# Transposes of a normalised token tile behind the next tile's matmuls, and the first products of the gated MLP interleaved over three units

## The chip, the core and the metric

One core of a Trainium2 chip runs the whole layer as one program. The metric is the device time of one execution in microseconds (us), of which the median of several runs counts. The engines each work through a queue of their own, in order: PE multiplies and transposes into banks of PSUM, ACT (ScalarE), DVE (VectorE) and POOL (GpSimd) do the elementwise work, and SP issues the DMA transfers. PE, ACT, DVE and POOL wait for each other only where one needs what another makes, or a buffer that another still uses.

## What is computed

The reference is one decoder layer on 1024 tokens of width 1024, in float32. The second half is the part that matters here:

```python
mix = jnp.concatenate([a_out, b_out], axis=-1)         # 1024 x 1024
x = x + rms_norm(mix @ w_out, norm_mix_post)
h = rms_norm(x, norm_ffn_pre)
g = jax.nn.gelu(causal_dwconv(h @ w_gate, conv_w, conv_b))   # width 2816
y = (g * (h @ w_up)) @ w_down
x = x + rms_norm(y, norm_ffn_post)
```

## The kernel before

The matrices are multiplied in parts: every operand is split into a high part (`fp32r`, written by ACT or DVE, L73 or L77) and a low part (the rest, L78, on DVE or POOL), and a product is three matmuls: high by high, high by low, low by high. One matmul is 128x128 by 128x512.

**The output projection.** The tokens are eight tiles of 128, taken in the order `TO` = 0, 1, 2, 3, 4, 6, 5, 7 (L682). For each tile, `wout_mm` issues 48 matmuls y (L622) into two banks. `wout_end` then normalises: ACT squares both halves (L698), POOL makes the statistics (L152, L157: n_7m and the first n_7r for tile 7), DVE scales (two L702) and adds x (L703), ACT squares the sum (L706), POOL makes the second statistics (L143, L145, again called n_7m and n_7r), and DVE scales the tile into xb (L708). `h2_trans` has PE transpose xb in eight 128x128 pieces (hT, L720), and ACT evacuates them with the gain (eight L725) into the tiles stg. `store_x1` stores the tile. In the loop the transposes of the previous tile stand before the last six of a tile's 48 matmuls (L1086).

**The gated MLP.** A unit is (gate or up, p): w_gate's or w_up's columns 256 p to 256 p + 255. Units come as g0, u0, g1, u1, ..., 22 in all; below, a, b and c are g0, u0 and g1, and 6a is product 6 of unit a. Each unit is one level of a fast matrix product with seven products, numbered 1 to 7; each is 12 matmuls (L845 to L847 in `prod`) with its own left side (hs, a split or a sum of stg, made by `hsplit` and `hs_sums`, L78 and L761 to L764) and its own weights (wtg or wtu, split by `wsplit`; the sums tg and tu of `tsums`, L795 to L798, two on POOL and two on DVE). Products 1 and 2 need only the even tiles (so tile 6 comes before tile 5), the others the odd ones too. The products go into banks A (1, then 2), B (6, then 7), C (5, then 3) and E (4), which the trace shows as Ag, Bg, Cg, Eg for gate units and Au, ... for up units. Between the two products of a bank `evac` reads the intermediate sum, and the second product has to wait for that. After product 3 of a gate unit `conv` does the convolution and GELU (L896 to L900), and `store_c` stores the result with four more sums for the down projection (sD, L911).

**What sets the order.** PE and SP run in the order of the code (`manual_schedule`); for ACT, DVE and POOL a scheduler chooses the order when the program is built, and from then on their queues are fixed. The order of the products is the list `SEQ`: of units a, b and c the products 1 and 2 of each, then 4a 4b, then the rest of a, the rest of b and the rest of c; from the fourth unit on `ORDER` = 1, 6, 2, 7, 5, 4, 3. Weights are split three products ahead (`LOOK`). Tile 7's transposes are called ahead of 1c, the fifth product. 32 buffers (mp, `mtile`) and 13 others (bg, `btile`) are handed around among all these tiles.

Of the kernel before, what the change touches and what calls it, by code (L numbers as in the profile page):

```python
# [34 lines left out]
NT = T // 128  # L35
# [27 lines left out]
def build(tc, x, g1, g2, g3, g4, w_in, ln_g, ln_b, sp_w, sp_b, rel, w_out, w_gate, w_up,  # L63
# [28 lines left out]
    with tc.manual_schedule(engines={ET.PE, ET.SP}), \  # L92
# [685 lines left out]
        def load_half(u):  # L778
            HALF[u] = btile("wh%s%d" % u).rearrange("p (k c) -> p k c", k=KT)
            sp.dma_start(HALF[u], (w_gate if u[0] == "g" else w_up)[:, u[1] * 256:u[1] * 256 + 128]  # L780
                         .rearrange("(k q) c -> q k c", q=128))

        def wblk(u, l, j):
            if u not in RW:
                return HALF[u][:, 4 * l:4 * l + 4, :]
# [74 lines left out]
        def evac(u, n):  # L860
# [197 lines left out]
        SEQ = [(u, n) for u in U[:3] for n in (1, 2)] + [(u, 4) for u in U[:2]]  # L1058
        SEQ += [(u, n) for u in U[:2] for n in (6, 7, 5, 3)] + [(U[2], n) for n in (6, 7, 5, 4, 3)]
# [12 lines left out]
        for c in range(1, NT):  # L1072
# [27 lines left out]
        hs_sums(2, 3)  # L1100
        for j in range(2, LOOK):
            wsplit(*SEQ[j])
        loaded = 2
        LS_ = len(SEQ)
        PRE = {LS_ - 5: lambda: [ahead_l(x, True) for x in range(2)], LS_ - 3: lambda: [ahead_l(x, True) for x in range(2, LL)],
               LS_ - 2: lambda: [ahead_s(x) for x in range(LS)]}
        for j, (u, n) in enumerate(SEQ):
            if j == 0:
                tsums(U[0])
            if j == 1:  # L1110
                tsums(U[1])
            if j == 4:
                h2_trans(NT - 1, bD)
                store_x1(NT - 1)
                for a in (4, 6, 7):
                    hsplit(a, 0, 3)
# [16 lines left out]
            if n == 7 and u[0] == "g" and u[1] > 0:  # L1133
# [93 lines left out]
```

## Time and profile before

| | us |
|---|---|
| median of 3 runs | 1215.32 (1213.35 to 1216.31) |
| profiled execution, its own time | 1219.78 |
| its span | 1218.1 |
| PE busy | 1163.5 (96%) |
| DVE busy | 840.5 (69%) |
| ACT busy | 581.8 (48%) |
| POOL busy | 368.1 (30%) |

PE's busy time counts matmuls as they overlap, so 96% is not 96% of its peak. The profile gives each engine's instructions with their start, what ended the idle time ahead of an instruction, and the TensorE clock granted in each stretch (1.00 is 2.4 GHz, 0.50 is 1.2 GHz). The output projection's tiles 1 to 7 lie between 470 and 562 us, the products of units a, b and c between 562 and 634 us, the remaining units up to about 1000 us, and the down projection behind them.

### The profile page before, as it was taken

To read this page: it belongs to the slowest core of one execution; us is meant where nothing else is said; L and a number is where in the kernel's file an instruction comes from. 1 tells how busy PE (TensorE), PEld (TensorE's weight loads), DVE (VectorE), ACT (ScalarE), POOL (GpSimd) and SP (SyncE) were. 2 spreads that over 40 slices of the span, in tenths; PEclk is the share of its full clock that TensorE was granted. 3 is DMA by queue.
4 is the path that set the end of the run, shared out by engine and by line. 5 is a ranking of instruction groups with operands and counts; after the bars stand their busy time and mean duration, and the time that the engine had idled before them with its cause. 6 is when DMAs were issued, how large, how long until landed. Compare 5 with 4: busy or idle time off the path is not lost.

```text
span 1218.1 us, 16548 instructions
## 1 busy us (share of the span) xinstructions
PE 1163.5 (96%) x5687; PEld 975.0 (80%) x5687; DVE 840.5 (69%) x1559; ACT 581.8 (48%) x1172; POOL 368.1 (30%) x401
## 2 busy tenths in 40 slices
PE   6899999999999999987899999999999999999996
PEld 4789978888887877875678888888888888888884
DVE  5752257777777785457777777677776779679665
ACT  4532156676765664445532434324343245445521
POOL 3850022333333473234023133221332220000342
PEclk9999999999998999999999999999999999999999
DMA  5314033433242232330223133231443279334336
GB/s 193 105 59 110 2 81 76 120 87 77 74 114 71 88 122 70 133 127 34 70 96 104 62 129 129 96 104 61 129 129 96 70 260 378 122 96 121 106 119 225
DMA packets 107562, 135.35 MB, mean 111 GB/s; under 512 B 30794, under 2 KB 74326, under 8 KB 107478
## 3 DMA queue, kind: packets, MB, share of 16 engines
q1 hardware_dynamic: 105318, 132.46, 34.9%
q10 hardware_dynamic: 2160, 1.84, 0.4%
q8 instruction: 45, 0.74, 0.3%
q14 instruction: 39, 0.32, 0.1%
HBM read 99.35 MB, written 35.71 MB: 111 GB/s over the span
## 4 chain that ended last, share of the span: by engine, by line
PE 77%; DVE 6%; issue 5%; POOL 5%; DMA 3%; ACT 2%; SPq 1%; POOLq 0%; DVEq 0%; ACTq 0%
PE d L986 15%; PE qk L471 10%; PE o L565 4%; PE pt L543 3%; PE s L511 2%; PE s L512 2%; PE v L240 2%; PE v L242 2%; PE v L241 2%; PE Bg L845 2%; PE Cu L845 2%; PE Bg L847 2%; PE Cu L846 2%; PE Cu L847 2%; PE Bg L846 2%
## 5 line engine op out<-in xcount | busy, mean ns | idle before, releaser
L986 PE MATMUL d<-t,s 128*128 128x512 f32 x924 | 210.3, 389 | 1.8 <-ACT t L73 1.5
L986 PEld LDWEIGHTS d<-t,s 128*128 128x128 f32 x924 | 173.3, 188 | 38.7 <-ACT t L73 1.9
L523 POOL TENSOR_SCALAR row<-row,rz 128x128 f32<-128x128 f32 (+3 forms) x96 | 72.8, 759 | 214.2 <-DVE rz L522 194.3
L520 ACT ACTIVATE row<-row,nm 128x128 f32<-128x128 f32 (+3 forms) x96 | 74.4, 775 | 48.9 <-DVE nm L515 48.6
L548 DVE TENSOR_TENSOR ptl<-pt,pth 128x512 fp32r<-128x512 f32 (+1 forms) x120 | 75.7, 634 | 20.1 <-ACT pth L547 18.5
L622 PE MATMUL y<-woh,ms 128*128 128x512 f32 x256 | 83.5, 398 | 1.5 <-POOL ms L78 1.1
L547 ACT ACTIVATE pth<-pt 128x512 fp32r<-128x512 f32 (+1 forms) x120 | 65.8, 550 | 34.0 <-PE pt L543 32.8
L471 PE MATMUL qk<-hTh,wqh 128*128 128x512 f32 x192 | 81.3, 423 | 0.0
L73 ACT ACTIVATE s<-sf 128x512 fp32r<-128x512 f32 x77 | 48.2, 627 | 66.4 <-PE d L986 26.1
L471 PE MATMUL qk<-hTl,wqh 128*128 128x512 f32 x192 | 78.9, 411 | 0.0
L471 PE MATMUL qk<-hTh,wql 128*128 128x512 f32 x192 | 76.9, 400 | 0.0
L78 DVE TENSOR_TENSOR s<-sf,s 128x512 fp32r<-128x512 f32 x77 | 56.5, 734 | 23.3 <-ACT s L73 23.1
L543 PE MATMUL pt<-ident,row 128*128 128x128 f32 x432 | 68.4, 275 | 1.8 <-POOL row L523 1.7
L1001 POOL TENSOR_TENSOR x<-x,g4t 128x512 f32<-128x512 f32 x12 | 18.8, 1577 | 162.1 <-DMA g4t<-in_norm_ffn_post 133.5
L73 ACT ACTIVATE wtg<-tg 128x512 fp32r<-128x512 f32 x44 | 27.5, 629 | 80.9 <-PE Cu L847 69.7
L898 DVE SCALAR_TENSOR_TENSOR c<-G,cols,c 128x1023 f32<-128x1023 f32 (+1 forms) x44 | 58.4, 1344 | 7.0 <-ACT c L896 7.0
L515 DVE CUSTOM_DVE_ANT_0 row<-s,bias 128x384 f32<-128x384 f32 (+2 forms) x96 | 49.8, 519 | 18.1 <-PE s L512 13.0
L543 PEld LDWEIGHTS pt<-ident,row 128*128 128x128 f32 x432 | 51.4, 140 | 10.7 <-POOL row L523 2.7
L73 ACT ACTIVATE wtu<-tu 128x512 fp32r<-128x512 f32 x44 | 27.6, 630 | 66.8 <-PE Cg L847 59.2
L795 POOL TENSOR_TENSOR tu<-wu 128x512 f32<-128x512 f32 x11 | 14.2, 1289 | 149.9 <-PE Ag L847 119.8
L622 PEld LDWEIGHTS y<-woh,ms 128*128 128x128 f32 x256 | 48.3, 189 | 12.2 <-POOL ms L78 1.6
L565 PE MATMUL o<-ptl,V 128*128 128x256 f32 x240 | 49.6, 288 | 4.8 <-DVE ptl L548 4.6
(334 smaller groups left out, 3224.4 us busy)
## 6 DMA issues: line engine op xcount, KB each, us to landing
sf<-sD SPq DMA_DIRECT2D x77, 256.0 KB, 2.8
wg<-in_w_gate SPq DMA_DIRECT2D x11, 1024.0 KB, 5.9
wu<-in_w_up SPq DMA_DIRECT2D x11, 1024.0 KB, 5.0
wd<-in_w_down SPq DMA_DIRECT2D x22, 512.0 KB, 7.1
sD<-c SPq DMA_DIRECT2D x30, 256.0 KB, 6.3
gcop<-gd SPq DMA_DIRECT2D x12, 576.0 KB, 4.6
wqk<-in_w_in SPq DMA_DIRECT2D x24, 256.0 KB, 5.5
bias<-gcop SPq DMA_DIRECT2D x12, 512.0 KB, 3.8
```

What stands on the lines that cost most here:

```text
L73: act.activation(hi, src, AF.Copy)
L78: lo_eng.tensor_sub(lo, src, hi.bitcast(F))
L471: pe.matmul(st[hf], w, m, start=k == 0 and j == 0, stop=k == KT - 1 and j == 2)
L520: act.activation(t[:, :w], t[:, :w], AF.Exp, bias=nm, scale=-1.0, accum_out=z)
L523: pool.tensor_scalar(t[:, :w], t[:, :w], rz, 1.0, op0=OP.mult, op1=OP.mult)
L543: pe.transpose(p[:, a * 128:(a + 1) * 128], r[:, jj * 128:(jj + 1) * 128], ident)
L547: act.activation(hi[:, :n], p[:, :n], AF.Copy)
L548: dve.tensor_sub(lo[:, :n], p[:, :n], hi.bitcast(F)[:, :n])
L565: pe.matmul(ov, v, t[:, s], start=j == 0 and x == 0, stop=x == 1 and j == 2 * g + 1, skip_group_check=True)
L622: pe.matmul(YP[i, hf], m, w, start=k == 0 and j == 0, stop=k == KT - 1 and j == 2)
L898: dve.scalar_tensor_tensor(c[:, d:T], g[:, 0:T - d], col(2 - d, f), c[:, d:T], op0=OP.mult, op1=OP.add)
L986: pe.matmul(b, l, r, start=first and n in FIRST and q == 0, stop=last and n in LAST and q == 2, skip_group_check=True)
```

## The change

1. In the loop over tiles the transposes (and the store, and the load of the next x) come after all 48 matmuls of the next tile, not before its last six. In the last pass they are left out: tile 5's now come ahead of the second product of the MLP. Tile 7's are called ahead of the fifth, as before.
2. The normalisation of tiles 5 and 7 and the transposes of both are put ahead in the scheduler's choice (`high_priority`).
3. The first 21 products alternate between units a, b and c (`HEAD`); the sums of stg, the splits and the sums of weights are called at other places in that list.
4. Unit c's weights come as two halves of 128 columns, and not as a half and then the whole. The sums tu of unit b take buffers of mp, not of bg.
5. `store_c` is called two products later; evacuations that waited for `conv` are done first in, first out, and may be of any product of an up unit.

```diff
-        def load_half(u):
+        def load_half(u, j):
-            HALF[u] = btile("wh%s%d" % u).rearrange("p (k c) -> p k c", k=KT)
+            HALF[u, j] = btile("wh%s%d_%d" % (u + (j,))).rearrange("p (k c) -> p k c", k=KT)
...
-                TW[key] = (btile if u in U[:2] else mtile)("t%s%d_%d" % (u + (a // 2,))).rearrange("p (a k c) -> p a k c", a=2, k=4)
+                TW[key] = (btile if u == U[0] else mtile)("t%s%d_%d" % (u + (a // 2,))).rearrange("p (a k c) -> p a k c", a=2, k=4)
...
-            if n == 2 and nm == "u" and p not in CONV:
+            if nm == "u" and p not in CONV:
                 LATE.append((u, n))
...
-        SEQ = [(u, n) for u in U[:3] for n in (1, 2)] + [(u, 4) for u in U[:2]]
-        SEQ += [(u, n) for u in U[:2] for n in (6, 7, 5, 3)] + [(U[2], n) for n in (6, 7, 5, 4, 3)]
+        HEAD = "1a 1b 2a 1c 2b 2c 4a 6a 6b 7a 5a 7b 3a 4b 6c 5b 7c 5c 3b 4c 3c".split()
+        SEQ = [(U["abc".index(x[1])], int(x[0])) for x in HEAD]
         SEQ += [(u, n) for u in U[3:] for n in ORDER]
...
-            for x_, f in enumerate(wout_mm(i, range(KT), bS if c % 2 else bD)):
-                if x_ == 42:
-                    h2_trans(TO[c - 1], bP)
-                    store_x1(TO[c - 1])
-                    if c + 1 < NT:
-                        load_xb(TO[c + 1])
-                    if c == 6:
-                        hsplit(1, 2, 4)
-                        hsplit(2, 2, 4)
+            for f in wout_mm(i, range(KT), bS if c % 2 else bD):
                 f()
-            wout_end(i)
+            if c < 6:
+                wout_end(i)
+            else:
+                with tc.high_priority(400):
+                    wout_end(i)
+            if c + 1 < NT:
+                h2_trans(TO[c - 1], bP)
+                store_x1(TO[c - 1])
+                load_xb(TO[c + 1])
+            if c == 6:
+                hsplit(1, 2, 4)
+                hsplit(2, 2, 4)
...
         for j, (u, n) in enumerate(SEQ):
-            if j == 0:
+            if j == 1:
+                with tc.high_priority(400):
+                    h2_trans(TO[NT - 2], bD)
+                store_x1(TO[NT - 2])
                 tsums(U[0])
-            if j == 1:
-                tsums(U[1])
+                hs_sums(2, 3)
+                hsplit(4, 0, 3)
+            if j == 2:
+                load_half(U[2], 1)
+                hsplit(6, 0, 3)
+                hsplit(7, 0, 3)
             if j == 4:
-                h2_trans(NT - 1, bD)
+                with tc.high_priority(400):
+                    h2_trans(NT - 1, bD)
                 store_x1(NT - 1)
-                for a in (4, 6, 7):
-                    hsplit(a, 0, 3)
                 hsplit(4, 3, 4)
                 hs_sums(3, 4)
                 hsplit(6, 3, 4)
                 hsplit(7, 3, 4)
+                tsums(U[1])
                 hsplit(5, 0, 4)
                 hsplit(3, 0, 4)
...
-            if n == 7 and u[0] == "g" and u[1] > 0:
+            if n == 4 and u[0] == "g" and u[1] > 0:
                 store_c(u[1] - 1)
```

Lines in the changed kernel move by one or two: L795 to L798 become L797 to L800, L845 becomes L847, L867 becomes L869, L896 to L900 become L898 to L902.

In the rows below, hT5 is the transposes of tile 5, hs4_1_0 the low part (1) of the first half (0) of the left side of product 4, wtg0_6 and wtu0_6 the weights of product 6 of units a and b (wtg1_6 of unit c), tg0 and tu0 the sums of a's and b's weights, yb7 and xb7 the tiles of token tile 7.

PE behind the last y of tile 7, before; the first matmul of each product is shown, eleven more follow it:

```order
L845 MATMUL Ag0_6364<-hs1_0_0_6124,wtg0_1_6338 128x512
...
L845 MATMUL Ag0_6364<-hs2_0_0_6132,wtg0_2_6341 128x512
...
L845 MATMUL Au0_6405<-hs1_0_0_6124,wtu0_1_6352 128x512
...
L845 MATMUL Au0_6405<-hs2_0_0_6132,wtu0_2_6361 128x512
...
L720 MATMUL hT7_0_6435<-ident_74,xb7_6213 128x128 x4
L720 MATMUL hT7_1_6444<-ident_74,xb7_6213 128x128 x4
L845 MATMUL Ag1_6517<-hs1_0_0_6124,wtg1_1_6385 128x512
...
L845 MATMUL Ag1_6517<-hs2_0_0_6132,wtg1_2_6402 128x512
...
L845 MATMUL Eg0_6552<-hs4_0_0_6454,wtg0_4_6420 128x512
...
L845 MATMUL Eu0_6568<-hs4_0_0_6454,wtu0_4_6514 128x512
...
L845 MATMUL Bg0_6586<-hs6_0_0_6462,wtg0_6_6532 128x512
```

The same place after the change:

```order
L847 MATMUL Ag0_6331<-hs1_0_0_6124,wtg0_1_6319 128x512
...
L720 MATMUL hT5_0_6346<-ident_74,xb5_6102 128x128 x4
L720 MATMUL hT5_1_6355<-ident_74,xb5_6102 128x128 x4
L847 MATMUL Au0_6390<-hs1_0_0_6124,wtu0_1_6322 128x512
...
L847 MATMUL Ag0_6331<-hs2_0_0_6132,wtg0_2_6325 128x512
...
L847 MATMUL Ag1_6443<-hs1_0_0_6124,wtg1_1_6328 128x512
...
L720 MATMUL hT7_0_6458<-ident_74,xb7_6239 128x128 x4
L720 MATMUL hT7_1_6467<-ident_74,xb7_6239 128x128 x4
L847 MATMUL Au0_6390<-hs2_0_0_6132,wtu0_2_6387 128x512
...
L847 MATMUL Ag1_6443<-hs2_0_0_6132,wtg1_2_6423 128x512
...
L847 MATMUL Eg0_6554<-hs4_0_0_6379,wtg0_4_6440 128x512
...
L847 MATMUL Bg0_6570<-hs6_0_0_6407,wtg0_6_6519 128x512
```

Tile 5's transposes have come from ahead of the last y to behind 1a, the two products of a bank are no longer neighbours, and between hT7 and 6a stand three products (2b, 2c, 4a) in place of four (1c, 2c, 4a, 4b).

DVE around L703 of tile 7, before:

```order
L763 TENSOR_TENSOR stg0_0_1_5610<-hsum1_6145,stg0_0_1_5610 128x2x128
L797 TENSOR_TENSOR tu0_1_6382<-wu0_6011 128x512
L703 TENSOR_TENSOR yb7_6318<-yb7_6318,xb7_6213 128x1024
L78 TENSOR_TENSOR wtg0_4_6420<-tg0_1_6358,wtg0_4_6420 128x512
L764 TENSOR_TENSOR stg0_1_1_5621<-stg0_1_1_5621,stg0_0_1_5610 128x2x128
L796 TENSOR_TENSOR tu0_0_6379<-wu0_6011,tu0_0_6379 128x512
L78 TENSOR_TENSOR hs4_1_0_6455<-stg1_1_0_5733,hs4_0_0_6454 128x2x384
L78 TENSOR_TENSOR hs4_1_1_6459<-stg1_1_1_5734,hs4_0_1_6458 128x2x384
L78 TENSOR_TENSOR hs6_1_0_6463<-stg0_0_0_5609,hs6_0_0_6462 128x2x384
L78 TENSOR_TENSOR hs6_1_1_6467<-stg0_0_1_5610,hs6_0_1_6466 128x2x384
L708 TENSOR_SCALAR xb7_6213<-yb7_6318,n3_7r_6335 128x1024
```

After the change:

```order
L703 TENSOR_TENSOR yb7_6299<-yb7_6299,xb7_6239 128x1024
L798 TENSOR_TENSOR tg0_0_6365<-wg0_6009,tg0_0_6365 128x512
L761 TENSOR_TENSOR hsum0_6140<-stg1_0_0_5748,stg1_1_0_5759 128x2x128
L761 TENSOR_TENSOR hsum1_6145<-stg1_0_1_5749,stg1_1_1_5760 128x2x128
L762 TENSOR_TENSOR stg1_0_0_5748<-stg0_0_0_5635,stg1_0_0_5748 128x2x128
L762 TENSOR_TENSOR stg1_0_1_5749<-stg0_0_1_5636,stg1_0_1_5749 128x2x128
L763 TENSOR_TENSOR stg0_0_0_5635<-hsum0_6140,stg0_0_0_5635 128x2x128
L763 TENSOR_TENSOR stg0_0_1_5636<-hsum1_6145,stg0_0_1_5636 128x2x128
L764 TENSOR_TENSOR stg0_1_0_5646<-stg0_1_0_5646,stg0_0_0_5635 128x2x128
L78 TENSOR_TENSOR hs4_1_0_6380<-stg1_1_0_5759,hs4_0_0_6379 128x2x384
L764 TENSOR_TENSOR stg0_1_1_5647<-stg0_1_1_5647,stg0_0_1_5636 128x2x128
L708 TENSOR_SCALAR xb7_6239<-yb7_6299,n3_7r_6316 128x1024
```

The sums of stg for tile 5 have moved between L703 and L708 of tile 7, and three long splits of hs and the sums tu have moved behind L708; the low part of wtg0_6 is the 22nd row behind L708 before, and the 29th after.

POOL at the same place, before:

```order
L798 TENSOR_TENSOR tg0_1_6358<-wg0_6009,tg0_0_6355 128x512
L795 TENSOR_TENSOR tu0_0_6379<-wu0_6011 128x512
L798 TENSOR_TENSOR tu0_1_6382<-wu0_6011,tu0_0_6379 128x512
L143 TENSOR_SCALAR n3_7m_6333<-ssc7_6331 128x1
L145 TENSOR_TENSOR n3_7r_6335<-n3_7m_6333,half_79 128x1
```

After the change:

```order
L797 TENSOR_TENSOR tg0_0_6365<-wg0_6009 128x512
L800 TENSOR_TENSOR tg0_1_6368<-wg0_6009,tg0_0_6365 128x512
L143 TENSOR_SCALAR n3_7m_6314<-ssc7_6312 128x1
L145 TENSOR_TENSOR n3_7r_6316<-n3_7m_6314,half_79 128x1
L797 TENSOR_TENSOR tu0_0_6497<-wu0_6011 128x512
L800 TENSOR_TENSOR tu0_1_6500<-wu0_6011,tu0_0_6497 128x512
```

The sums tu have moved from ahead of tile 7's second statistics to directly behind them; one sum of tg is still ahead.

## Rows read from the trace of the kernel before

**Rows 1.** The page, part 1: engine, busy us, share of the span, instructions.

```profile
PE 1163.5 (96%) x5687; PEld 975.0 (80%) x5687; DVE 840.5 (69%) x1559; ACT 581.8 (48%) x1172; POOL 368.1 (30%) x401
```

**Rows 2.** Waits of PE, 465 to 760 us: total us, times, longest.

```profile
PE hT L720 <- DVE xb L708: 10.0, 4, 4.1
PE Bg L845 <- DVE tmpg L867: 1.8, 2, 0.9
PE Bu L845 <- DVE tmpu L867: 1.6, 1, 1.6
PE Ag L845 <- ACT tmpg L864: 1.4, 2, 0.7
...
```

**Rows 3.** Busy time by stretch: length, engines' busy us, granted clock, DMA share, GB/s.

```profile
640.00:960.00 320.00, 320.00 (x1414) 264.96 (x1413) 240.56 (x306) 122.62 (x175) 95.80 (x66) 1.00 0.32 103
```

**Rows 4.** Timeline of PE: start us, us, line, operation, count [idle before <- releaser].

```profile
527.13 1.09 PE L720 MATMUL hT<-ident,xb 128*128 128x128 f32 x8 [1.08 <-DVE xb L708]
542.13 1.09 PE L720 MATMUL hT<-ident,xb 128*128 128x128 f32 x8 [2.99 <-DVE xb L708]
558.25 1.97 PE L720 MATMUL hT<-ident,xb 128*128 128x128 f32 x8 [4.11 <-DVE xb L708]
561.88 0.39 PE L845 MATMUL Ag<-hs,wtg 128*128 128x512 f32 x1
576.75 1.10 PE L720 MATMUL hT<-ident,xb 128*128 128x128 f32 x8 [1.87 <-DVE xb L708]
577.60 0.48 PE L845 MATMUL Ag<-hs,wtg 128*128 128x512 f32 x1
626.25 0.39 PE L845 MATMUL Cg<-hs,wtg 128*128 128x512 f32 x1
634.41 0.39 PE L845 MATMUL Au<-hs,wtu 128*128 128x512 f32 x1
```

**Rows 5.** Busy time and granted clock behind the third of these waits.

```profile
558.00:561.00 3.00, 2.75 (x11) 2.56 (x12) 0.79 (x2) 1.60 (x7) 0.00 (x0) 0.50 0.00 0
```

**Rows 6.** Timeline of DVE.

```profile
556.45 1.74 DVE L708 TENSOR_SCALAR xb<-yb,n_5r 128x1024 f32<-128x1024 f32 x1 [1.52 <-POOL n_5r L145]
564.36 1.41 DVE L702 SCALAR_TENSOR_TENSOR yb<-y,n_7r,g2t 128x512 f32<-128x512 f32 x2 [0.44 <-POOL n_7r L157]
569.36 0.41 DVE L764 TENSOR_TENSOR stg<-stg,stg 128x256 f32<-128x256 f32 x1
569.70 0.68 DVE L796 TENSOR_TENSOR tu<-wu,tu 128x512 f32<-128x512 f32 x1
570.30 3.55 DVE L78 TENSOR_TENSOR hs<-stg,hs 128x768 fp32r<-128x768 f32 x4
575.94 0.75 DVE L708 TENSOR_SCALAR xb<-yb,n_7r 128x1024 f32<-128x1024 f32 x1 [2.09 <-POOL n_7r L145]
585.11 1.22 DVE L78 TENSOR_TENSOR hs<-hsum,hs 128x1024 fp32r<-128x1024 f32 x1
586.25 0.41 DVE L78 TENSOR_TENSOR hs<-stg,hs 128x256 fp32r<-128x256 f32 x1
```

**Rows 7.** Timeline of POOL.

```profile
556.38 1.26 POOL L795 TENSOR_TENSOR tg<-wg 128x512 f32<-128x512 f32 x1
570.52 4.48 POOL L798 TENSOR_TENSOR tu<-wu,tu 128x512 f32<-128x512 f32 x1 [3.70 <-DVE tu L796]
575.08 0.19 POOL L143 TENSOR_SCALAR n_7m<-ssc 128x1 f32<-128x1 f32 x1
```

**Rows 8.** Timeline of ACT: evacuation of one tile's transposes.

```profile
542.82 2.17 ACT L725 ACTIVATE stg<-hT,cols 128x128 f32<-128x128 f32 x8 [2.44 <-PE hT L720]
```

**Rows 9.** DMA: landing time of one kind (the page), and issues a pair apart.

```profile
sD<-c SPq DMA_DIRECT2D x30, 256.0 KB, 6.3
661.48 2.57 SPq L911 DMA_DIRECT2D sD<-c  x3
699.56 0.57 SPq L911 DMA_DIRECT2D sD<-c  x1
```

More of the change, by code (lines that the diff above doesn't have):

```diff
@@ L776, in build @@
         HALF = {}
-        def load_half(u):
-            HALF[u] = btile("wh%s%d" % u).rearrange("p (k c) -> p k c", k=KT)
-            sp.dma_start(HALF[u], (w_gate if u[0] == "g" else w_up)[:, u[1] * 256:u[1] * 256 + 128]
+        def load_half(u, j):
+            HALF[u, j] = btile("wh%s%d_%d" % (u + (j,))).rearrange("p (k c) -> p k c", k=KT)
+            c0 = u[1] * 256 + j * 128
+            sp.dma_start(HALF[u, j], (w_gate if u[0] == "g" else w_up)[:, c0:c0 + 128]
                          .rearrange("(k q) c -> q k c", q=128))
         def wblk(u, l, j):
-            if u not in RW:
-                return HALF[u][:, 4 * l:4 * l + 4, :]
+            if (u, j) in HALF:
+                return HALF[u, j][:, 4 * l:4 * l + 4, :]
             return RW[u][:, 4 * l:4 * l + 4, j, :]
@@ L902, in conv @@
             while LATE:
-                evac(*LATE.pop())
+                evac(*LATE.pop(0))
         def store_c(p):
@@ L1084, in build @@
                 hs_sums(0, 2)
-            for x_, f in enumerate(wout_mm(i, range(KT), bS if c % 2 else bD)):
-                if x_ == 42:
-                    h2_trans(TO[c - 1], bP)
-                    store_x1(TO[c - 1])
-                    if c + 1 < NT:
-                        load_xb(TO[c + 1])
-                    if c == 6:
-                        hsplit(1, 2, 4)
-                        hsplit(2, 2, 4)
-                f()
-            wout_end(i)
-        for j in range(2):
+            for f in wout_mm(i, range(KT), bS if c % 2 else bD):
+                f()
+            if c < 6:
[10 more added lines that the diff above has]
+                hsplit(2, 2, 4)
+        for j in range(LOOK):
             wsplit(*SEQ[j])
[L1100 to L1103, printed above, removed]
+        loaded = 3
         LS_ = len(SEQ)
-        PRE = {LS_ - 5: lambda: [ahead_l(x, True) for x in range(2)], LS_ - 3: lambda: [ahead_l(x, True) for x in range(2, LL)],
+        PRE = {LS_ - 5: lambda: [ahead_l(x, True) for x in range(2)],
+               LS_ - 3: lambda: [ahead_l(x, True) for x in range(2, LL)],
                LS_ - 2: lambda: [ahead_s(x) for x in range(LS)]}
         for j, (u, n) in enumerate(SEQ):
-            if j == 0:
+            if j == 1:
+                with tc.high_priority(400):
+                    h2_trans(TO[NT - 2], bD)
+                store_x1(TO[NT - 2])
                 tsums(U[0])
-            if j == 1:
-                tsums(U[1])
+                hs_sums(2, 3)
[4 more added lines that the diff above has]
+                hsplit(7, 0, 3)
             if j == 4:
-                h2_trans(NT - 1, bD)
+                with tc.high_priority(400):
+                    h2_trans(NT - 1, bD)
                 store_x1(NT - 1)
-                for a in (4, 6, 7):
-                    hsplit(a, 0, 3)
                 hsplit(4, 3, 4)
@@ L1124, in build @@
                 wsplit(*SEQ[j + LOOK])
-                if SEQ[j + LOOK][1] == 3 and loaded < len(U):
+                if SEQ[j + LOOK][1] == 3 and SEQ[j + LOOK][0] != U[2] and loaded < len(U):
                     load_gu(U[loaded])
```

2 lines of the change are left out of this document (1 added, 1 removed).

## Prediction, before the changed kernel was run

> **What bounds the kernel now.** The page first: TensorE is busy 96% of the span, VectorE 69% [rows 1]. So only its pauses can be won, and the change touches one stretch. The table of waits says where they are: from 465 us to 760 us PE idled 10.0 us in four waits of the transposes hT for VectorE's L708, and the rest in short waits of a product, nearly all for the evacuation of the bank that it adds to: Bg 1.8, Bu 1.6 and Ag 1.4 us, and five more groups of 0.7 to 1.1 us (4.4 in all, 1.1 of it in code that stays) [rows 2]. The table by stretches closes the region: from 640 to 960 us PE is busy 320.00 of 320.00 us, whatever VectorE does [rows 3]. What the head of the MLP gains is therefore kept, and the end is shifted by it. I take the start of Au of unit u1 (the fourth unit), 634.41 us, as the mark: 252 matmuls of units a, b and c are then done [rows 4].
>
> **Part 1: the transposes up to tile 7.** The waits were 1.08 (tile 4), 2.99 (tile 6), 4.11 (tile 5) and 1.87 us (tile 7) [rows 4]. After the 4.11 the granted clock was 0.50, the lower of its two levels (1.2 GHz), from 558 to 561 us [rows 5]: from hT at 558.25 to the first Ag at 561.88 it took 3.63 us for a block of transposes (0.85 at the full clock, 576.75 to 577.60) and six matmuls (36 take 8.16, from 626.25 to 634.41, so 1.36) [rows 4], a loss of 1.4.
> For tiles 0 to 6 the block now stands six matmuls, 1.4 us, later. That alone covers tile 4's wait. For tile 6 it leaves 1.6, but ScalarE now squares a tile before it evacuates the previous one's transposes (eight L725, 2.17 us [rows 8]), so tile 6's statistics and its L708 come about 2 us earlier: nothing is left, with some 1 us in hand. Tile 5's block stands behind y of tile 7 and twelve products, 18 matmuls or 4.1 us later; L703 of tile 5 comes ahead of the weight splits, its L708 near 549.5, its slot near 554. I set all three waits to zero. Their cover is VectorE having room before 551 us; if the priority moved nothing, tile 6 and 5 would give back 1 to 2 us.
> Products therefore start at 561.88 − 8.18 − 1.4 − 0.85 (hT of tile 5 has moved behind them) = 551.45 us, 10.4 earlier.
>
> **Part 2: what is late next.** PE now needs, until 6a (Bg of unit a), 84 matmuls and two blocks of transposes, 19.1 + 1.7 us: it could reach 6a at 572.3. VectorE decides whether it may, so I walk its new queue with durations of before [rows 6], taking the distance between starts: 0.60 for a 128x512 operation, 0.34 for 128x256, 0.89 for 128x768, 1.14 for 128x1024, 0.67 for each half of L702.
> L702 of tile 7 started 2.5 us after the first Ag (561.88 to 564.36 [rows 4, 6]); now it can at 551.45 + 2.5 = 553.9. Behind it: two L702 and L799 to 555.85, L703 to 557.0, L798 to 557.6, seven 128x256 sums, one 128x768 split and another sum to 561.2. Then L708 of tile 7, which needs POOL's n_7r.
> POOL is the doubtful part. Its L800 for tg stands ahead of n_7m and n_7r and is released at 557.6 by L798, when VectorE runs eight or nine operations without a break. In before such a sum took 4.48 us, where another took 1.26: it began at 570.52 beside four splits that ended at 573.85 and ended 1.15 us after them [rows 7]. So I let it run only when VectorE stops at L708, 561.2 to 562.5 us; n_7m and n_7r, 0.86 from the start of the one to L708 (575.08 to 575.94 [rows 6, 7]), bring 563.35. Directly behind n_7r POOL now has L797 for tu. The like pair stood in before for tile 5: L795 started at 556.38, and L708 took 1.74 instead of 0.75 [rows 6, 7]. L708 of tile 7 then ends at 565.0, and PE, at hT7 by 563.2, waits 2 us.
> The Trainium skill, SBUF — State Buffer, section "Who interferes with whom", calls the port pair that VectorE and GpSimd share an exclusive lock: whichever starts first holds it for its whole instruction, and a VectorE instruction with two SBUF inputs contends with a GpSimd one that reads SBUF. By that rule both collisions come, as taken here; without it L708 ends at 561.9 and the gain below is some 5 us greater. The trace agrees (4.48 and 1.74 us), but shows each only once.
> From L708 of tile 7 to the low half of 6a's weights, wtg0_6, VectorE's queue has 29 rows: five of 128x768 (4.45), fourteen of 128x256 (4.76), four of 128x1024 (4.56), six of 128x512 (3.6): 17.4 us. It has wtu0_2, wtg1_2, wtg0_4 and two sums for tu in it, because three units are started at once; PE has 36 matmuls, 8.2 us, and one block for the same time. So VectorE becomes the bound: wtg0_6 is there at 565.0 + 17.4 = 582.4, and PE has idled before 2c (for wtg1_2, some 3.5 us) and at the third matmul of 6a (the first with a low weight half, some 4 us). The clock loss of the first pause is hidden in the second; the second I charge as the 4.11 us wait was, 1.5.
>
> **Part 3: from 6a to the mark.** 166 matmuls are left, 37.8 us. The waits for evacuations go, since another unit's product, 2.7 us, now stands between two that share a bank, and the longest of these waits was 1.6 [rows 2]. One may return: with the convolution of unit a in its queue VectorE evacuates 6c about 0.7 us after 7c could start; with its start-up 0.8. Mark: 582.4 + 37.8 + 1.5 + 0.8 = 622.5, against 634.41: a gain of 11.9 us.
> At nothing I cost: loading unit c in two halves (SP issues the second when y of tile 7 frees its buffer, near 552 us, and the first reader, a sum on POOL, comes behind the evacuation of 5a, 40 us on), and calling the stores of c two products later, which nobody reads before the down products.
> The profiled execution took 1219.78 us (span 1218.1), 4.5 above the median; I expect it near 1207.9, and the median, 1215.32, near 1203.4.
> **Bounds of the unknown costs.** Best: POOL never held up, 561.9 + 17.4 = 579.3, no clock loss, 0.3 of evacuation: 617.4, gain 17.0. Worst: POOL's second sum for tu takes a further 1.3 from VectorE, the ping-pong of ScalarE and VectorE over the splits adds a tenth of 17.4, clock twice (3.0) and evacuations 1.5: 582.4 + 1.3 + 1.7 + 37.8 + 3.0 + 1.5 = 627.7, gain 6.7. I take 11.9, since both collisions have a row of their own.
>
> **Rivals.**
> *No collision.* POOL finds gaps between VectorE's operations: 1215.3 − 17.0 = 1198.3. For it: where POOL's sum started first it ran its 1.26 [rows 7], and a break of VectorE of a few tenths at 557.6 would let it start first. Against it: the 4.48, begun in just such a place.
> *VectorE keeps up.* PE is never held after 551.45: 551.45 + 1.7 + 57.3 (252 matmuls) = 610.4, gain 24.0, 1191.3. For it: VectorE is busy only 69% of the span [rows 1]. Against it: 17.4 us of queue for 9 of PE.
> *The waits only move.* Tile 6 or 5 still waits 1 to 2 us and the head loses the worst sum's amounts: gain 5 to 7, 1208.5 to 1210.
> *It doesn't do what it says*, since hT5 and hT7 still wait as long as before, because L708 of both is late with its statistics: of some 8 us of short waits about 4 come back before 6a and 0.8 later: some 3 us, 1212.
> *Slower.* The place is the steady part, nine pairs of units. In the changed kernel the tiles c, G and tmp of a pair take over buffers of stores to sD of an earlier pair, and wait for those transfers; before most did not. If such a wait fell on VectorE or ScalarE just ahead of a split, each pair would lose up to the landing time of 6.3 us [rows 9]. It decides from 11.9 / 9 = 1.3 us a pair; at 2 us a pair the time is 1215.3 − 11.9 + 18 = 1221. Against it: the buffers are those of stores a whole pair back, and a pair lasts 38.1 us (661.48 to 699.56 [rows 9]), several times the landing.
>
> **How the numbers follow.** Forecast 0.52 (its own range 1199.5 to 1207), no collision 0.20, VectorE keeps up 0.06, the waits only move 0.13, it doesn't do what it says 0.05, slower 0.04. The range from 1196.5 to 1209.5 holds the first two and most of the fourth, about 0.82. A measurement here can tell about 0.3%, 3.6 us, from no change. Faster by more: the first four, 0.90, less a little for the upper end of the fourth: 0.89. Within: 0.07. Slower: 0.04. The time is the forecast's, 1203.4.
>
> **What would show it.** Right: no wait of hT for L708 of tiles 4, 5 and 6, products starting near 551.5; a wait of about 2 us or less at hT7; POOL's L800 for tg far longer than 1.3 us; two new waits of Ag and Bg for wtg by L78, together 6 to 9 us; the granted clock at 0.50 behind one of them; the mark near 622; 80 of 80 us busy beyond. Wrong: waits of y or hT before 551 us (Part 1), no wait for wtg (Part 2, gain 17 or more), pauses of PE after the mark (the slower rival).

## Result, and the profile after

The changed kernel took 1200.9 us (four runs, 1200.5 to 1204.0) beside 1215.8 for the kernel before (four runs): a ratio of 0.9884 with a 95% interval of 0.9860 to 0.9909, 1.2% faster. In two later calls it gave 1204.4 and 1203.2 us, ratios 0.9904 (0.9890 to 0.9919) and 0.9892 (0.9875 to 0.9909). The median of its twelve runs is 1203.6 us; the forecast was 1203.4. As gains, call by call, these are 14.9, 11.9 and 13.0 us, where the forecast had 11.9.

The profiled execution took 1203.99 us (span 1202.3), 15.8 less than before's. The page, part 1, in the columns of [rows 1]:

```profile
PE 1160.8 (97%) x5687; PEld 975.2 (81%) x5687; DVE 841.0 (70%) x1559; ACT 582.2 (48%) x1172; POOL 380.2 (32%) x401
```

The busy times are those of before to within 3 us, POOL's apart; what went is idle time of PE. Its waits from 465 to 760 us, as in [rows 2]:

```profile
PE Ag L849 <- DVE wtg L78: 3.3, 1, 3.3
PE Bg L849 <- DVE wtg L78: 1.5, 1, 1.5
PE Bg L847 <- DVE tmpg L869: 1.0, 1, 1.0
PE Au L849 <- DVE wtu L78: 0.9, 1, 0.9
PE Bg L847 <- ACT wtg L73: 0.3, 1, 0.3
PE hT L720 <- DVE xb L708: 0.3, 1, 0.3
```

The 10.0 us of hT have become 0.3, and of the evacuations one is left (1.0, product 7c). In their place stand waits that before did not have: for the low halves of the splits for 2c (3.3), 6a (1.5) and 2b (0.9). The places in PE's timeline, in the columns of [rows 4]:

```profile
547.63 0.39 PE L847 MATMUL Ag<-hs,wtg 128*128 128x512 f32 x1
559.91 1.07 PE L720 MATMUL hT<-ident,xb 128*128 128x128 f32 x8 [0.34 <-DVE xb L708]
568.66 0.74 PE L849 MATMUL Ag<-hs,wtg 128*128 128x512 f32 x1 [3.27 <-DVE wtg L78]
578.10 0.50 PE L849 MATMUL Bg<-hs,wtg 128*128 128x512 f32 x1 [1.46 <-DVE wtg L78]
605.08 0.47 PE L847 MATMUL Bg<-hs,wtg 128*128 128x512 f32 x1 [1.02 <-DVE tmpg L869]
618.80 0.39 PE L847 MATMUL Au<-hs,wtu 128*128 128x512 f32 x1
```

The first product starts at 547.63 (before 561.88), and the mark, Au of u1, at 618.80 (before 634.41). Three stretches, in the columns of [rows 3]:

```profile
569.00:572.00 3.00, 3.00 (x8) 2.32 (x8) 3.00 (x10) 2.42 (x4) 3.00 (x1) 0.50 0.02 5
580.00:582.00 2.00, 2.00 (x6) 1.52 (x6) 0.00 (x0) 0.00 (x0) 0.99 (x1) 0.50 0.00 0
620.00:900.00 280.00, 280.00 (x1237) 231.73 (x1235) 212.65 (x269) 110.02 (x156) 84.91 (x58) 1.00 0.33 107
```

The granted clock is at its lower level (0.50) behind each of the two waits for splits. Beyond the mark PE is busy 280.00 of 280.00 us, as in [rows 3], so what the head gains is kept: from the mark to the end of the span it is 583.5 us, before 583.7.

VectorE's and GpSimd's rows at the places of [rows 6] and [rows 7]:

```profile
549.62 1.41 DVE L702 SCALAR_TENSOR_TENSOR yb<-y,n_7r,g2t 128x512 f32<-128x512 f32 x2 [2.81 <-POOL n_7r L157]
559.01 0.75 DVE L708 TENSOR_SCALAR xb<-yb,n_7r 128x1024 f32<-128x1024 f32 x1 [2.09 <-POOL n_7r L145]
560.55 1.77 DVE L78 TENSOR_TENSOR wtu<-wu,wtu 128x512 fp32r<-128x512 f32 x1
577.37 0.68 DVE L78 TENSOR_TENSOR wtg<-tg,wtg 128x512 fp32r<-128x512 f32 x1
```

```profile
553.51 4.56 POOL L800 TENSOR_TENSOR tg<-wg,tg 128x512 f32<-128x512 f32 x1 [2.66 <-DVE tg L798]
559.66 2.12 POOL L797 TENSOR_TENSOR tu<-wu 128x512 f32<-128x512 f32 x1 [0.68 <-PE Ag L849]
568.17 12.81 POOL L800 TENSOR_TENSOR tu<-wu,tu 128x512 f32<-128x512 f32 x1 [6.40 <-DVE tu L798]
```

The sum L800 for tg was held up for 4.56 us, L708 of tile 7 stood 2.09 us behind it, the next sum cost the split wtu 1.1 us, and wtg0_6, the split that 6a waits for, ends at 578.05.

### The profile page after: what moved, and what is told of

Same layout as the page of the kernel before. It is cut to its first block, busy times and chain, and to the rows that moved or that the text cites. A ratio compares the mean times of both kernels' runs of the same rounds, so it can differ in the third digit from the quotient of the medians.

```text
span 1202.3 us, 16542 instructions
## 1 busy us (share of the span) xinstructions
PE 1160.8 (97%) x5687; PEld 975.2 (81%) x5687; DVE 841.0 (70%) x1559; ACT 582.2 (48%) x1172; POOL 380.2 (32%) x401
## 4 chain that ended last, share of the span: by engine, by line
PE 84%; DVE 6%; DMA 3%; POOL 2%; ACT 2%; issue 1%; SPq 1%; POOLq 0%; DVEq 0%; ACTq 0%
PE d L988 15%; PE qk L471 10%; PE y L622 7%; PE o L565 4%; PE pt L543 4%; PE s L511 2%; PE v L240 2%; PE s L512 2%; PE v L242 2%; PE v L241 2%; PE Bu L847 2%; PE Bu L849 2%; PE Bu L848 2%; PE Bg L849 2%; PE Bg L847 2%; PE Bg L848 2%
## 5 line engine op out<-in xcount | busy, mean ns | idle before, releaser
L797 POOL TENSOR_TENSOR tu<-wu 128x512 f32<-128x512 f32 x11 | 15.3, 1388 | 149.3 <-PE Ag L849 75.5
L900 DVE SCALAR_TENSOR_TENSOR c<-G,cols,c 128x1023 f32<-128x1023 f32 (+1 forms) x44 | 57.7, 1327 | 6.7 <-ACT c L898 6.7
```

## The experiments

Executions differ by 2 to 3 us ahead of the output projection and, as will be seen, at the very end. So beside the times stand two places in the profiled execution, counted from the same place in PE's order, the end of the 42nd matmul of y of tile 1, called the common matmul below (the start of the first block hT where the blocks have the old place, 1.36 us ahead of it where they stand six matmuls later). Without any waiting it would be 59.0 us from the first product to the mark (252 matmuls and two blocks, 57.3 and 1.7 us; in before and the order alone one block, 58.2).

| kernel | median us (runs) | ratio to before, 95% | first product | mark |
|---|---|---|---|---|
| before | 1215.8 to 1216.3 | 1 | 83.95 | 156.5 |
| changed | 1200.9, 1204.4, 1203.2 (4 each) | 0.9884, 0.9904, 0.9892 | 72.0 | 143.2, 141.7, 141.7 |
| transposes only | 1205.1, 1204.5 (4 each) | 0.9908, 0.9900 | 72.0 | 144.1, 144.3 |
| order only | 1215.7 (10) | 0.9997 (0.9985 to 1.0009) | 81.0 | 155.5 |
| old place of tiles 0 to 6 | 1212.5 (10) | 0.9964 (0.9950 to 0.9978) | 79.0 | 151.4 |
| one sum on VectorE | 1204.4 (4) | 0.9904 (0.9889 to 0.9918) | 72.0 | 143.6 |
| late splits | 1197.7 (4) | 0.9843 (0.9826 to 0.9861) | 72.0 | 136.8 |
| late splits, one sum | 1197.0 (4) | 0.9842 (0.9826 to 0.9859) | 72.0 | 135.8 |
| the same, 4b behind 6c | 1195.3, 1195.4 (4 each) | 0.9835, 0.9822 (0.9806 to 0.9839) | 72.2, 72.0 | 134.8, 134.6 |
| transposes only, late splits | 1202.8 (4) | 0.9888 (0.9873 to 0.9902) | 72.0 | 143.1 |

**The transposes alone.** The kernel before with the changed loop over tiles, tile 5's block ahead of the second product and the priorities; the products in the old order:

```diff
             if j == 1:
+                with tc.high_priority(400):
+                    h2_trans(TO[NT - 2], bD)
+                store_x1(TO[NT - 2])
+                hs_sums(2, 3)
                 tsums(U[1])
             if j == 4:
-                h2_trans(NT - 1, bD)
+                with tc.high_priority(400):
+                    h2_trans(NT - 1, bD)
```

> Only the transposes' part: the blocks of transposes at their new places, tiles 5 to 7 with the priority, the products in the order of before. Theory A (the transposes' waits are the gain; the interleaving mainly pays for the room that their going takes away): no wait of hT for tiles 4, 6 and 5, first Ag near 547.6 us as in the changed kernel; VectorE's queue from L708 of tile 7 to the low half of 6a is some 15 us and PE has 10.9 us of products for it, so a wait of 3 to 4 us before 6a and a clock loss behind it, and before's short waits for evacuations stay: mark near 619 to 621, time 1201 to 1204. Theory B (without the interleaving the gain of the transposes goes back into waits for evacuations and splits): mark near 626, gain 7 to 9, time 1207 to 1209.

Beside the changed kernel once more, in one call:

> The transposes' part alone once more, beside the changed kernel. Its mark lay 13.7 us ahead of before's, 0.9 and 2.4 us behind the two profiles of the changed kernel. Theory A (the interleaving adds 1 to 2.5 us): 1 to 2.5 us slower than the changed kernel of this call. Theory B (it adds the 4 us by which the medians of the first calls differed): 3.5 to 4.5 us slower. Theory C (it adds nothing that can be measured): within 0.7 us.

> The changed kernel, unchanged, for a comparison in one call with the transposes' part alone, with the late splits in the old order and with the best version. The marks of the two profiles so far lay 14.6 and 16.1 us ahead of before's (counted from the first block of transposes): time 1200 to 1204.5.

It took 1205.1 and 1204.5 us, and the mark was where theory A of the first run had it, but by another way. Waits of PE of the first run, 465 to 760 us:

```profile
PE Ag L845 <- ACT tmpg L864: 2.4, 1, 2.4
PE Bg L845 <- DVE tmpg L867: 1.8, 2, 0.9
PE Bu L845 <- DVE tmpu L867: 1.6, 1, 1.6
...
```

There is no wait at 6a: PE stood for evacuations (the 2.4 is ScalarE's copy behind its splits, in before 0.7) and so came to 6a after VectorE. In one call it was 1204.5 to the changed kernel's 1203.2; the intervals of the two overlap, the marks lie 0.9 to 2.6 us apart. So the transposes, with the priorities, bring 11 to 12 of the changed kernel's 12 to 15 us, and the interleaving adds 1 to 2.6 by the marks. What the priorities bring by themselves wasn't tried.

**The order alone.** The changed kernel with the loop of before (transposes ahead of the last six matmuls, tile 5's in the last pass) and without priorities:

> Only the order of the products over three units (with what belongs to it: unit c loaded in two halves, the store of c two products later); the transposes stand where before has them, without priority. Theory A: the four waits of the transposes stay (8.2 us before the first Ag, which starts near 561.9), hT7 waits 2 to 3 us; VectorE has worked ahead in those waits, so 6a waits 1 us or less, and the waits for evacuations go: mark 625 to 628, gain 6 to 9, time 1206 to 1209: so the gains of the two parts add up to more than the whole. Theory B (the order adds VectorE work at the wrong place): waits for wtg of 3 us or more come here too, gain 0 to 3, time 1212 to 1215.

No gain at all, which neither theory had for the right reason. PE, VectorE, GpSimd and ScalarE at tile 7:

```profile
574.97 1.97 PE L720 MATMUL hT<-ident,xb 128*128 128x128 f32 x8 [7.03 <-DVE xb L708]
```

```profile
574.16 0.75 DVE L708 TENSOR_SCALAR xb<-yb,n_7r 128x1024 f32<-128x1024 f32 x1 [0.75 <-POOL n_7r L145]
```

```profile
564.84 6.19 POOL L800 TENSOR_TENSOR tg<-wg,tg 128x512 f32<-128x512 f32 x1 [1.83 <-DVE tg L798]
```

```profile
571.06 0.63 ACT L73 ACTIVATE wtg<-tg 128x512 fp32r<-128x512 f32 x1 [4.69 <-POOL tg L800]
...
572.08 1.05 ACT L706 ACTIVATE xb<-yb 128x1024 f32<-128x1024 f32 x1
```

PE came to hT7 4.8 us sooner: 2.9 of it ahead of the first product, where tile 5's block waited 0.90 us and not 4.11, the rest mainly because the two waits for evacuations ahead of hT7 were gone. And it waited 7.0 instead of 1.9: L708 of tile 7 came 98.3 us after the common matmul, in before 98.0 (575.94 [rows 6] less 477.93). A wait that was taken out came back at the next place, as the rival "the waits only move" has it for other tiles. That L708 came no earlier has a cause of this kernel: the sum for tg was held up for 6.19 us, ScalarE's split of it waited 4.69 us for the sum, and L706 of tile 7 stood behind that split in ScalarE's queue. In the changed kernel, which has the priority, L706 runs at 553.06 us, ahead of such a split. So a part of "no gain" can be the missing priority; the new order with the priority and with every block at its old place wasn't run. Behind hT7, 6a waited a further 3.1 us for its weights (1.66 and 1.48), about what theory B had.

**The place of the blocks of tiles 0 to 6.** The changed kernel with

```diff
-            for f in wout_mm(i, range(KT), bS if c % 2 else bD):
+            for x_, f in enumerate(wout_mm(i, range(KT), bS if c % 2 else bD)):
+                if x_ == 42 and c + 1 < NT:
+                    h2_trans(TO[c - 1], bP)
+                    store_x1(TO[c - 1])
+                    load_xb(TO[c + 1])
                 f()
```

> The changed kernel with the blocks of tiles 0 to 6 six matmuls earlier, at the place of before; tile 5's block stays behind the first product. Theory A (the six matmuls, 1.4 us, are what tiles 1 to 4 and 6 gained): waits of 0.2 us at tiles 1 to 3 and 1.1 at tile 4 come back, tile 6 waits about 1.3; first Ag 2.5 to 3.5 us later, near 550.5; VectorE's queue behind L708 of tile 7 moves with it: time 1203 to 1204.5. Theory B (ScalarE's squares ahead of the evacuations did it, the place is worth nothing): no wait of tile 6, less than 1 us back, 1201 to 1202.

Both theories were too small: 1212.5 us, the first product 7 us later, the mark 8 to 10. The waits of tiles 4 and 6 are back to the hundredth, 1.08 and 2.99 us, and behind the second the granted clock falls; these waits, 0.2 to 0.3 us more for each tile and the lower clock are the 7 us. PE and the stretch behind it:

```profile
540.52 1.70 PE L720 MATMUL hT<-ident,xb 128*128 128x128 f32 x8 [2.99 <-DVE xb L708]
```

```profile
540.00:543.00 3.00, 2.48 (x11) 2.28 (x12) 0.47 (x1) 1.59 (x7) 0.00 (x0) 0.64 0.50 176
```

The first square of tile 6 on ScalarE, here and in the changed kernel:

```profile
528.23 0.65 ACT L698 ACTIVATE yb<-y 128x512 f32<-128x512 f32 x1
```

```profile
523.60 0.60 ACT L698 ACTIVATE yb<-y 128x512 f32<-128x512 f32 x1 [3.05 <-PE y L622]
```

Counted from the common matmul these are 51.9 and 48.0 us, and L708 of the tile is 4.0 us earlier too. Some 2.1 of that is what tiles 1 to 4 no longer lose ahead of it. At tile 1, where nothing has been lost yet, the first square comes 1.8 us earlier (0.88 us behind the common matmul, not 2.65): 0.9 because the block of transposes no longer stands ahead of the last six y, 0.9 because ScalarE now squares ahead of the eight L725. Beside this stands the 1.36 us of the place itself. They come together and weren't tried apart.

This kernel has the priorities and tile 5's block at its new place, and the order alone has neither: 1212.5 against 1215.7 us, the mark 4.0 us earlier. So with the other blocks at their old place these two are together worth some 3 to 4 us.

**One sum on VectorE.** `tsums` of unit a does its last sum, held up for 4.56 us, on VectorE:

```diff
-            pool.tensor_sub(tw(u, 3), wblk(u, 1, 0), tw(u, 1))
+            (dve if u == U[0] else pool).tensor_sub(tw(u, 3), wblk(u, 1, 0), tw(u, 1))
```

> The changed kernel with one operation moved: the last of the four sums for unit a's tg runs on VectorE instead of GpSimd. Theory A (the hold-up of that sum delays n_7r and so L708 of tile 7, behind which VectorE's whole queue stands): no gap of 2.1 us ahead of L708, which comes 1.4 to 2 us earlier (near 557.2 where the first product is at 547.6), the added row costs 0.6: the wait at 2c falls from 3.3 to about 2, mark 1.4 us earlier: time 1199 to 1200. Theory B (VectorE's rows only fill the gap in another order, L708 is not what counts): the queue's end moves by nothing, or by the 0.6 of the added row to the late side: 1200.5 to 1201.5.

> The changed kernel once more, unchanged, as the companion of the next three and for a second profile of the same order of work. If the hold-up of GpSimd's sum for tg (4.56 us) is the order's, it comes again, with hT7 waiting some 0.3 us, 2c 3.3 us and 6a about 1.8; if it hangs on the start of one execution, the sum takes about 1.3 us in this one. Time 1199.5 to 1203.5 either way.

1204.4 us both. With the sum on VectorE L708 did come 2.7 us earlier (8.7 us after the first product instead of 11.4), and the wait of hT7 went; but 2c then waited for longer. Waits of PE:

```profile
PE Ag L849 <- DVE wtg L78: 4.6, 1, 4.6
...
```

VectorE had lost the time elsewhere: 0.72 us in a gap ahead of L708 (GpSimd's n_7m took 1.34 us there and 0.19 in the first profile of the changed kernel), 1.15 us in a gap ahead of L798, 1.1 us in a split, and 0.6 us for the added row. The second profile of the unchanged kernel shows the like. There the same sum started just ahead of VectorE's next row and ran in 1.34 us:

```profile
551.26 1.34 POOL L800 TENSOR_TENSOR tg<-wg,tg 128x512 f32<-128x512 f32 x1 [2.66 <-DVE tg L798]
...
557.42 6.69 POOL L797 TENSOR_TENSOR tu<-wu 128x512 f32<-128x512 f32 x1 [3.79 <-PE Ag L849]
```

```profile
551.04 1.86 DVE L761 TENSOR_TENSOR hsum<-stg,stg 128x256 f32<-128x256 f32 x2
555.70 0.74 DVE L708 TENSOR_SCALAR xb<-yb,n_7r 128x1024 f32<-128x1024 f32 x1
564.15 0.69 DVE L798 TENSOR_TENSOR tu<-wu,tu 128x512 f32<-128x512 f32 x1 [1.16 <-POOL tu L797]
565.36 1.77 DVE L78 TENSOR_TENSOR wtg<-tg,wtg 128x512 fp32r<-128x512 f32 x1
...
```

L708 was early here too, 10.3 us after the first product. But VectorE paid elsewhere: 1.1 us in a sum, 1.16 in a gap, 1.1 in a split, 3.4 in all; in the first profile it was 2.09 and 1.1, 3.2. The third profile of it goes as the second: 1.35 us for the sum, L708 10.3 us after the first product, the mark at 141.7. So the theory that L708 decides falls. What decides is the end of VectorE's queue: from L702 of tile 7 to the end of wtg0_6 it is 28.4 and 28.6 us in the first two profiles, and 28.9 with the sum on VectorE. What GpSimd's operations cost VectorE, 2.9 to 3.4 us, is paid somewhere in it, whichever operation is hit.

**Late splits.** The changed kernel with what 6a doesn't need moved behind it: the splits for products 7, 5 and 3 are called with the weight splits of later products (those of 7 whole), the sums for tu with unit b's first split that needs them:

```diff
                 hsplit(6, 0, 3)
-                hsplit(7, 0, 3)
...
                 hsplit(6, 3, 4)
-                hsplit(7, 3, 4)
-                tsums(U[1])
-                hsplit(5, 0, 4)
-                hsplit(3, 0, 4)
             if j + LOOK < len(SEQ):
                 wsplit(*SEQ[j + LOOK])
+                if j == 5:
+                    hsplit(7, 0, 4)
+                if j == 6:
+                    hsplit(5, 0, 4)
+                if j == 8:
+                    hsplit(3, 0, 4)
```

> The changed kernel with work that 6a doesn't need moved behind it in VectorE's queue: the splits hs of products 7, 5 and 3 are called after the weight splits of 6b, 7a and 7b, the sums for tu with the first weight split of unit b. Theory A (VectorE's queue between L708 of tile 7 and 6a sets when PE goes on): two 128x768 and more rows go ahead of wtg1_2, six rows of 128x768 to 128x1024 ahead of wtg0_6, 6 us in all: the wait of 3.3 us at 2c falls to about 1.6, the one at 6a goes, half of the clock losses too: mark 613 to 614.5, time 1195 to 1197. Theory B (another thing sets 2c and 6a, the units' loads or ScalarE's high halves, or the moved splits are late themselves at 7a, 5a and 3a): within 2 us of the changed kernel's 1200.9.

1197.7 us, 0.7 beyond theory A's range, with the mark 4.9 to 6.4 us earlier (at 611.0 in this execution, 2 us ahead of its range, 1.4 of them because the execution reached the common matmul earlier): theory A. Waits of PE, and the stretch with the longest but one of them:

```profile
PE Bg L847 <- DVE tmpg L869: 1.7, 1, 1.7
PE Bg L848 <- DVE hs L78: 1.4, 1, 1.4
...
```

```profile
567.00:570.00 3.00, 1.70 (x8) 1.08 (x6) 3.00 (x8) 2.79 (x6) 3.00 (x1) 1.00 0.00 0
```

The wait at 2c is gone altogether; 6a still waits 1.4 us, now for a split of its left side. The clock stays at 1.00 through the head, so of 6.4 us (against the first profile of the changed kernel) 3.6 are waits and the other 2.8 mainly the two stretches at the lower clock.

**The same in the old order of the products** (in the kernel with the transposes alone the splits of 7, 5 and 3 are called three products later, with the weight splits of 7a, 5a and 3a; the sums for tu stay where they were):

> The transposes' part alone, in the old order of the products, with the late splits (hs of products 7, 5 and 3 called three products later). Theory A (in the old order PE waits for evacuations of banks, 9 us in all, and hardly for VectorE's splits; so late splits help there only by the 1.2 to 1.5 us of 4b's wait): mark 1 to 2 us earlier than without them, 1202 to 1204; the interleaving is then worth 5 to 7 us once VectorE's queue is relieved, and little before. Theory B (late splits give the same 6 us in either order, the interleaving is worth the same 1 to 2.5 us in both): 1197.5 to 1199.

1202.8 us; the mark 1.0 to 1.2 us earlier than without late splits. Its waits are those for evacuations, as in theory A:

```profile
PE Bg L845 <- DVE tmpg L867: 2.8, 2, 2.0
PE Bu L845 <- DVE tmpu L867: 1.6, 1, 1.6
PE Au L845 <- ACT tmpu L864: 1.5, 1, 1.5
...
```

So the interleaving is worth 6.3 us by the marks (5 by the times, which come from two calls) once VectorE's queue is relieved, and 1 to 2.6 as it stands.

**A version that beats both.** Late splits with the sum on VectorE, and then with 4b behind 6c, so that two products stand between 6c and 7c, which share a bank:

```diff
-        HEAD = "1a 1b 2a 1c 2b 2c 4a 6a 6b 7a 5a 7b 3a 4b 6c 5b 7c 5c 3b 4c 3c".split()
+        HEAD = "1a 1b 2a 1c 2b 2c 4a 6a 6b 7a 5a 7b 3a 6c 4b 5b 7c 5c 3b 4c 3c".split()
```

> Late splits (as in the run e5_late_splits) and the sum for tg on VectorE together. In the run of the late splits GpSimd's two sums each lengthened a row of VectorE by 1.1 us ahead of L708, hT7 waited 0.4 us and 6a 1.4 us for its splits. Theory A: L708 comes about 1 to 2 us earlier, both waits go: 1.5 us less than with the late splits alone, 1195.5 to 1196.8. Theory B (the wait at 6a is set by ScalarE, which evacuates hT7 and splits the high halves): the wait at 6a stays at 1 us or more, 1197 to 1198.5.

> The run before it with one more step: 4b comes behind 6c instead of ahead of it, so that two products (5.4 us) lie between 6c and 7c, which share a bank. Theory A (7c waits for VectorE's evacuation of 6c, which stands in the queue behind the convolution of unit a: 1.0 us in the changed kernel, 1.7 with late splits): that wait goes, 1 to 1.7 us less than the run before it: 1194 to 1195.5. Theory B (the weights of 6c, four sums and a split, come three us too late for a place so early): a wait for wtg at 6c of 1 to 3 us, no gain or a loss: 1196 to 1198.

> The changed kernel with late splits, the sum for tg on VectorE and 4b behind 6c, once more (as in the run e8_all), in one call with the changed kernel. Its mark lay 23.1 us ahead of before's, 7 to 8.4 more than the changed kernel's: 1194 to 1197, 6 to 9 us faster than the changed kernel of this call.

With the sum 1197.0 us, 1.0 us less by the mark, nothing that the times can tell, and 6a still waits 1.25 us: for VectorE's split of its left side, not for ScalarE, so neither theory was right about it. With 4b behind 6c 1195.3 and 1195.4 us: the wait at 7c is gone. In one call with the changed kernel (1203.2) it is 7.8 us faster, 1.8% faster than before. What is left is, but for two waits of 0.3 us, that of 6a. Waits of PE in the last of these runs:

```profile
PE Bg L848 <- DVE hs L78: 1.2, 1, 1.2
...
```

## Why the prediction was right, and where it was off

**The bound and the mark.** As forecast: the gain lies in PE's pauses ahead of the mark, and the "slower" rival is dead (no pause in 280 us behind it). Counted from the common matmul the sum had the mark at 144.6 us (73.5 to the first product, 31.0 to 6a, 40.1 from there); the first profile has 143.2 (72.0, 30.5, 40.7), the second 141.7 (72.0, 30.6, 39.1).

**Part 1: the mechanism right, the gain a seventh too small.** No wait was left for tiles 4, 6 and 5. Counted from the common matmul the first product came 11.9 us earlier, the sum had 10.4. The step that was short is the size of the waits: I took PE's rows, four waits. In before the weight loads waited for L708 at seven blocks. Who waited for L708 there, us and times:

```profile
  PEld hT L720: 13.2, 7
  PE hT L720: 10.0, 4
```

At tile 1 it looked like this, L708 and the block behind it:

```profile
489.12 0.75 DVE L708 TENSOR_SCALAR xb<-yb,n_1r 128x1024 f32<-128x1024 f32 x1 [2.13 <-POOL n_1r L145]
```

```profile
489.93 1.09 PE L720 MATMUL hT<-ident,xb 128*128 128x128 f32 x8
```

hT follows the end of L708, 489.87, yet has no wait in brackets. A tile took 12.0 us (477.93 to 489.93), in the changed kernel 11.8 (476.96 to 488.75); 0.2 to 0.3 us at each of six tiles are the missing 1.5. The room at tile 6 was smaller than the sum had it. The 2 us by which its L708 was to be earlier were 1.8, as tile 1 shows, and in the changed kernel L708 of tile 6 ended only 0.15 us ahead of its block (which began at 535.86), where I had some 1 us in hand:

```profile
534.95 0.76 DVE L708 TENSOR_SCALAR xb<-yb,n_6r 128x1024 f32<-128x1024 f32 x1 [0.72 <-POOL n_6r L145]
```

**Part 2: the sum right, its parts not.** From L702 of tile 7 to the end of wtg0_6 the prediction had 28.5 us; the first two profiles have 28.4 and 28.6. In the first the hold-up of tg's sum came as taken, 4.56 us, ended by VectorE's stop at L708. The second collision did not hit L708: the sum for tu had to wait for PE to be done with 1c (0.68 us, its buffer), and lengthened the split wtu behind it, for which PE then stood 0.92 us at 2b, a wait that I hadn't forecast. So hT7 waited 0.34 us, not 2, and the queue behind L708 took 18.3, not 17.4. The waits at 2c and 6a were 3.3 and 1.8 where I had 3.5 and 4: together 5.1, less than the 6 to 9 that I had named as a sign of being right. PE reached the third matmul of 6a 30.5 us after the first product, where I had 30.95. That the end fits is in part luck: I had the price of GpSimd's sums, some 3 us (2.15 ahead of L708 and 1.0 in it), but not where VectorE would pay it, and in the other two profiles it paid only 1.1 us ahead of L708, in a sum, and the rest behind it. The clock was charged once, 1.5 us; in the first profile it fell twice, in the second once, which is most of the 1.5 us between their marks.

One reading of before was short. I took the 1.74 us of L708 as the only such collision there; a 128x256 sum of VectorE (L763, at 565.69 us) took 1.41 us instead of 0.41 beside GpSimd's sum L795 for tu, which had started at 565.52. So the trace of before already showed that shorter rows pay the same.

The page of the Trainium skill that I drew on, SBUF — State Buffer, section "Who interferes with whom", says that issue order decides who blocks. The runs bear it out: the same sum for tg, in the same place of the program, was held up for 4.56 us in one execution and ran 1.34 us in another, in which VectorE's row took 1.1 us more. But the result that I hung on it, 5 us more without collisions, is not to be had by moving the one sum: the collisions moved on (2.9 us, and 0.6 for the added row, where the first two profiles of the changed kernel have 3.2 and 3.4) and the time stayed.

**Part 3.** 40.7 us from 6a to the mark in the first profile and 39.1 in the second, where I had 40.1; the one evacuation wait was forecast 0.8 and measured 1.0, at 7c, as named.

**What the sum did not tell.** It gives the whole, and not what each part is worth by itself: the transposes with the priorities bring 11 to 12 us, the order without them 0.2 us, both 12 to 15. Part 3 has the waits for evacuations as gone and Part 2 the waits at 2c and 6a as new; set against the transposes alone, the runs show that the second take back most of the first (waits of PE from the first product to the mark: 9.3 and 10.5 us with the transposes alone, 7.0 to 7.4 in the changed kernel).

**The rest of the profiled execution.** Of its 15.8 us, 13.3 are the head (156.5 to 143.2). Some 2.3 lie ahead of it: about 1 before the output projection, and a wait of y for POOL's ms, 1.12 us, that before has and the changed kernel has not. POOL's first statistic there, before and after:

```profile
467.14 2.13 POOL L152 TENSOR_SCALAR n_0m<-ssb 128x1 f32<-128x1 f32 x1 [7.09 <-ACT yb L698]
```

```profile
466.10 0.19 POOL L152 TENSOR_SCALAR n_0m<-ssb 128x1 f32<-128x1 f32 x1 [7.09 <-ACT yb L698]
```

The long row and the wait came in the profiles of before and of the order alone, in none of the other twelve; nothing was tried on it, and the cause stays open.

## What to carry to other kernels

Before a wait is counted as gained, follow the engine that ends it to the next thing that PE needs from it: here VectorE's queue from tile 7 to the first product of sums was 28 to 29 us long whatever happened in it, and only taking rows out of it (late splits) moved the end. A reordering that gives PE work during one wait is worth little while the same chain ends the next wait (1 to 2.6 us here), and more once that chain is shorter (6.3 us), so try the parts alone and together. Wait tables of the matmul rows leave out what weight loads wait for: compare the pitch of a loop with its work.

## What the runs showed of the hardware

- A 128x512 sum of GpSimd took 1.3 us by itself and up to 12.81 us where it started behind VectorE's row in an unbroken run of VectorE's rows; where it started first, a row of VectorE took 1.1 us more than its usual time (0.75 to 1.86 for two sums, 0.68 to 1.77 for a split). In one program both came about, from one execution to the next. So here two engines waited for each other though neither needed what the other made, nor a buffer that it used.
- The last 48 matmuls of the program, which the change doesn't touch, took 11.8 us in six of the fourteen profiles and 13.0 to 14.4 in the others. The two profiles of the changed kernel that differ most:

```profile
1181.56 10.95 PE L988 MATMUL d<-t,s 128*128 128x512 f32 x47 [0.30 <-DVE t L78]
```

```profile
1179.02 14.10 PE L988 MATMUL d<-t,s 128*128 128x512 f32 x48 [1.63 <-ACT t L73]
```

  In the first the 48 begin one matmul ahead of its row, behind a wait of 1.16 us, and the granted clock was 1.00 from 1181 to 1186 us. In the second, waits of 0.65, 0.31 and 1.63 us for splits stand ahead of them, and the granted clock was 0.50 from 1179 to 1184 us. With the 2 to 3 us of the beginning this is most of the scatter of the totals, and why marks told more than medians here.
- Whether the granted clock fell behind a pause of PE can't be read from the pause's length in these runs. 1.4 us, PE busy 1.70 of 3 us, left it at 1.00 (late splits, 567 to 570 us), while in the changed kernel 0.35 and 1.46 us at 6a were followed by 0.50 (580 to 582 us). The same pause of 2.99 us ahead of tile 6's block was followed by 0.64 in the run with the old place of the blocks, as shown above, and by 1.00 in before:

```profile
542.00:545.00 3.00, 2.87 (x17) 2.53 (x18) 0.07 (x1) 2.18 (x9) 0.00 (x0) 1.00 0.37 146
```

  And of the two profiles of the transposes alone, with a pause of 2.4 us at the same product, the clock fell to 0.50 behind it in one and stayed at 1.00 in the other.
